# A decoder step on one core: six hidden groups of the third MLP block go from eight products of quarter matrices to seven, the cache stream's last steps move ahead of them, and its softmax is cut into portions

## The chip, the core and the metric

One Trainium2 chip, of which the program uses one core. The core has a matrix engine (TensorE, PE in the profile, with PEld for its weight loads), a vector engine (VectorE, DVE), an activation engine (ScalarE, ACT), a general engine (GpSimd, POOL) that also issues the gathers by index, and SyncE (SP), whose queue issues most plain DMAs. Each engine works through its own instructions in their order; semaphores tie the engines together. The metric is device time in microseconds for one execution. Three executions of the kernel before took 3270.63, 3259.38 and 3270.8 us, median 3270.63.

## The reference, cut to what matters

One inference step of a one-layer trunk. The new sequence (2048 tokens) and 64 sampled tokens (8 sequences of 8) go through one input projection, two kinds of attention, an output projection, a layer norm, an MLP and another layer norm:

```python
def _block_out(x, fox_h, m_h, og, mlstm_norm_w, w_o, ln1_g, ln1_b, w1, w2, ln2_g, ln2_b):
    ...
    x1 = _layer_norm(DN_ALPHA * x + mix, ln1_g, ln1_b)
    hid = jnp.square(jax.nn.relu(x1 @ w1))
    return _layer_norm(DN_ALPHA * x1 + hid @ w2, ln2_g, ln2_b)
```

`w1` is 1024 x 4096 and `w2` 4096 x 1024. The sampled tokens attend to a paged cache of 8192 keys and values for each of the 8 sequences:

```python
    s_past = jnp.einsum('bqhd,bkhd->bhqk', q, k_past).astype(jnp.float32) * scale
    s_past = s_past + Ln[..., :, None] + R[:, :, None, :]
    ...
    p = jax.nn.softmax(jnp.concatenate([s_past, s_new], axis=-1), axis=-1).astype(v_new.dtype)
    o = jnp.einsum('bhqk,bkhd->bqhd', p[..., :P], v_past) + jnp.einsum('bhqk,bkhd->bqhd', p[..., P:], v_new)
```

All is float32. The kernel splits each operand of a large product into a high and a low part and forms high x high, high x low and low x high: three matmuls for one product.

## The kernel before, in words

**Stages.** Phase A (to about 900 us) makes the input projection and the recurrent heads, phase B (to about 1320 us) the attention of the new sequence, phase O (to about 1560 us) the output projection and the first layer norm, phase C (to the end) the MLP. Phase C takes the tokens in four blocks: three of 512 tokens (tiles 0 to 3, 4 to 7, 8 to 11) in `phase_c`, and one of 512 tokens and the 64 sampled ones in `last_block`.

**A block of the MLP.** The 4096 hidden columns come in 16 groups `fc` of 256. `hidden(fc)` (L1560) loads and splits 256 columns of `w1`, forms 48 matmuls of 512 columns (2 halves of the group, 8 pieces of the inner dimension, 3 parts) and takes relu and square on ACT. `output([fc])` (L1578) forms the group's share of `hid @ w2`: 4 token tiles x 2 halves of the 1024 output columns x 2 halves of the group x 3 parts, again 48 matmuls of 512 columns, which DVE adds into the tiles' rows `y` (L1607). The two groups 14 and 15 are taken together, and the layer norm follows.

**Seven products.** `last_block` already uses another form for groups 0 to 13, the function `seven` (L1638), which stands unchanged in both kernels: the group's hidden values are seen as 2 x 2 quarters (two token halves, two hidden halves), the rows of `w2` as 2 x 2 quarters, and seven products of sums of quarters (Strassen's scheme in Winograd's form) replace eight. `sums(n)` forms the sums on POOL (four of 128x256, four of 128x512), `build(n)` splits them on ACT and DVE, `output(n)` forms the seven products, each 2 tiles x 3 parts = 6 matmuls of 512 columns, so 42 in place of 48, and `join()` adds the collected first product to the rows once at the end, in 12 DVE additions. `hidden(n)` there hands the low part of its second `w1` piece to POOL.

**The cache stream.** `sample_attention` is a generator: 295 steps `n` that gather a sequence's key pages (POOL), transpose them (DVE), form scores (`sQ` matmuls), take the softmax of a sequence once its scores are complete, transpose the weights into `PTs`, gather value pages, and form weights x values (`sO` matmuls, `pv_step`, L2120, 16 for each sequence, 8 matmuls each). For each `pv_step` two gathers of 512 KB fetch a pair of value pages (L2113). There are two places for such a pair: the tile `vt`, and `xr` (or `vx` in phase O); a place can be filled again when the `pv_step` that read it is done.

**What sets the order.** The stream is sewn into the other phases by `tick(us)` (L129): every unit of matrix work counts its nominal time, and for each `PACE_C` = 5 us of it in phases O and C one stream step is emitted, behind the work already emitted. In the third block, after `hidden(13)` and `output([12])`, a loop emits all steps that are left (L1627). `sampled()` (L1526) follows: it reads the stream's result back through HBM (`mixs` -> `dmix` -> `mxs`), splits it (`mhs`) and forms the output projection and first layer norm of the 64 sampled tokens, which the fourth block needs. A scheduler then arranges the emitted instructions on each engine; what it made is each engine's fixed order.

Of the kernel before, what the change touches and what calls it, by code (L numbers as in the profile page):

```python
# [10 lines left out]
F32 = mybir.dt.float32  # L11
F32R = mybir.dt.float32r
I32 = mybir.dt.int32
AF = mybir.ActivationFunctionType
# [7 lines left out]
PACE_B = float('inf')  # L22
PACE_C = 5
PACE_M = 2.3
D = 1024
# [27 lines left out]
def body(ctx, tc, I, O, stages):  # L53
# [111 lines left out]

    def layer_norm(x, np_, g, b, wk, tg, eng=None, by=None):
# [9 lines left out]
        (by or V).tensor_tensor(x, x, g[:np_], op=OP.mult)  # L176
        (eng or G).tensor_tensor(x, x, b[:np_], op=OP.add)
# [1333 lines left out]
    def phase_c():  # L1511
        es, es_h = ExitStack(), ExitStack()
        pc, ph = C["pc"], es_h.enter_context(tc.tile_pool(name="ph", bufs=1, side="right", reuse_waits="tile"))
# [33 lines left out]
        CB = [[0, 1, 2, 3], [4, 5, 6, 7], [8, 9, 10, 11], [12, 13, 14, 15, 16]]  # L1547
        def load(ci):
            for i, t in enumerate(CB[ci]):
                x1_turn(t, i, x1_row(t) if i == 3 else x1_load(t), lambda: ppc.tile([128, 4, 128], F32, name="px2", tag="ph", bufs=3))  # L1550
            vx["more"] = landing

        vx["more"] = landing
        for ci, blk in enumerate(CB[:3]):
# [4 lines left out]

            def hidden(fc):  # L1560
                w1p = C.pop("w1", None) or w1_pieces(fc)
                H[fc] = []
                for f in range(2):
                    h2 = ph.tile([128, 1024], F32R, name="h", bufs=4)
                    hh, hl = h2[:, 0:512], h2[:, 512:1024]
                    H[fc].append((hh, hl))
                    ps = ppc.tile([128, 512], F32, name="ph", tag="ph", bufs=3)
# [10 lines left out]
            def output(fcs):  # L1578
                w2p = [piece(w2[fc * 256 + k * 128:fc * 256 + k * 128 + 128].rearrange("(k p) c -> p k c", p=128)) for fc in fcs for k in range(2)]
                h = [x for fc in fcs for x in H.pop(fc)]  # L1580
                gb = gb2
                for t in blk:
# [8 lines left out]
                    both = 15 in fcs and t == blk[-1]  # L1591
                    pss = []
                    for hf, cs in enumerate(halves):
                        if not both or hf == 0:
                            todo = halves if both else [cs]
                            new = [ppc.tile([128, 512], F32, name="py", bufs=3) for _ in todo]
                            pss += new
# [14 lines left out]

            for fc in range(16):
                if fc == 14:
                    vx["more"] = None
                hidden(fc)
                if fc == 15:
                    take_back()
                    if ci == 2:
                        es_px.close()  # L1620
                        C["px"] = es_px.enter_context(tc.tile_pool(name="px", bufs=1, reuse_waits="tile"))
                        C["w"] = 576
                    load(ci + 1)
                if fc > 0:
                    output([14, 15] if fc == 15 else [fc - 1])
                if fc == 13 and ci == 2:
                    while acc[1] is not None:  # L1627
                        tick(100.0)
                    sampled()
                    gb2 = [ps_.tile([128, D], F32, name=f"{x}3", tag="vt", bufs=2) for x in "gb"]  # L1630
                    for v, x in zip(gb2, "gb"):
                        SY.dma_start(v, dap(I[f"ln2_{x}"], 0, [[0, 128], [1, D]]))
        es_h.close()
        es.close()
        last_block(w2, gb2)
        es_px.close()

# [119 lines left out]

    def last_block(w2, gb):
        es = ExitStack()
        ph = es.enter_context(tc.tile_pool(name="phs", bufs=1, side="right", reuse_waits="tile"))  # L1760
        ppl = es.enter_context(tc.tile_pool(name="ppl", bufs=1, space=PSUM, reuse_waits="tile"))
        T0, T1 = (12, 13), (14, 15)
# [93 lines left out]
def sample_attention(tc, I, O, ps_, pps, cst, ident, sqk, dnl, dR, dmix, dqb, vx, kx, pe, ring_a):  # L1856
# [180 lines left out]
    def softmax(b):  # L2037
# [20 lines left out]
        rp = z["rp"] = ps_.tile([128, 2, 5], F32, name="rp", bufs=2)  # L2058
        for u in range(4):
            for hg in range(2):  # L2060
                x = z["U"][u][:, hg].rearrange("p b k t -> p (b k t)")
                A.activation(x, x, AF.Exp, bias=m4[:, hg:hg + 1], accum_out=rp[:, hg, u:u + 1])
        for hg in range(2):
            A.activation(z["Sn"][:, hg], z["Sn"][:, hg], AF.Exp, bias=m4[:, hg:hg + 1], accum_out=rp[:, hg, 4:5])

    def softmax_new(b):

        z = state[b]
        rs = z["rs"] = ps_.tile([128, 2], F32, name="rs", bufs=2)
        V.tensor_reduce(rs, z["rp"], axis=AX.X, op=OP.add)  # L2070
        pn = z["pn"] = ps_.tile([8, 2, 32], F32, name="PTn", bufs=2)
# [14 lines left out]
    def weights(b, u, hg):  # L2086
# [6 lines left out]
        for f in range(4):  # L2093
            T.transpose(p[:, f], z["U"][u][:, hg, f].rearrange("p k t -> p (k t)"), ident)
        for f in range(4):
            (A.copy if f % 2 else V.tensor_copy)(PT[:, hg, f].rearrange("p g h q -> p h g q"),
                                                 p[:, f].rearrange("p (h g q) -> p h g q", g=4, q=8))

# [71 lines left out]
    def step(n):  # L2170
# [14 lines left out]
        if b is not None and b < 8:  # L2185
            softmax(b)
        due = (n - 38) // 2 if n > NA + 2 else (n - 39) // 2
        lead = 2
# [12 lines left out]
        if b is not None and b < 8:  # L2201
            softmax_sum(b)
        u = at(n, 37, 8)
        if u is not None and u < 32:
# [61 lines left out]
```

## Time and profile before

| | |
|---|---|
| median of three executions | 3270.63 us (3259.38 to 3270.8) |
| the profiled execution's own time | 3264.98 us |
| its span, first to last instruction | 3263.1 us |
| PE busy | 3174.9 us, 97% of the span, 20140 matmuls |
| DVE, ACT, POOL busy | 2230.5, 1393.6, 1049.9 us |
| mean granted TensorE clock | 0.990 |

The profile is one page and a trace behind it. A row on a group reads: line, engine, operation, output tile <- input tiles, shape, count | busy us, mean ns of one | idle time of the engine just before them, and what ended it. A row of a timeline reads: start us, duration us, engine, line, operation, and in brackets the idle time before it and its releaser. A row of a table of stages gives busy time and count of instructions for PE, PEld, DVE, ACT and POOL, then the granted clock, the DMA engines' busy share and GB/s. Matmul durations overlap (matmuls are pipelined), so the pace of PE is read from starts or from counts in a stretch. One execution's span and its own time differ by 1.9 us here.

### The profile page before, as it was taken

What the parts mean: (1) busy time and instruction counts of PE and PEld (TensorE: products, weight loads), DVE (VectorE), ACT (ScalarE), POOL (GpSimd) and SP (SyncE); (2) the same over time, 40 slices, a digit from 0 to 9 for tenths busy, and PEclk for the clock granted to TensorE, in tenths of its full rate; (3) what the DMA queues carried; (4) which work ended last, traced back from release to release, by engine and by line L of the source; (5) the groups of instructions that cost most, each with busy time, mean ns of one, the idle gap of its engine ahead of it and who ended that gap; (6) DMA issues with size and microseconds to landing.
All of it is one profiled execution on the core that took longest, in us unless ns stands there. A gap on an engine that the chain in (4) does not pass through costs nothing.

```text
span 3263.1 us, 54920 instructions
## 1 busy us (share of the span) xinstructions
PE 3174.9 (97%) x20140; PEld 2555.0 (78%) x20140; DVE 2230.5 (68%) x5239; ACT 1393.6 (43%) x2753; POOL 1049.9 (32%) x1171
## 2 busy tenths in 40 slices
PE   9999999999999999999999999999999999999998
PEld 8878787786777777777777777777777777799997
DVE  5857667666577777766566767666667545777777
ACT  4444244444377777412333333242423333454443
POOL 0011121432344444354333324323234210264441
PEclk9999999999999999999999999999999999999999
DMA  6565774977743224777686768776678645442221
GB/s 193 150 198 167 231 230 144 315 259 218 222 128 85 79 84 118 254 282 263 250 289 213 288 238 288 263 249 244 239 240 305 210 160 176 134 139 84 91 90 56
DMA packets 413845, 641.88 MB, mean 197 GB/s; under 512 B 83020, under 2 KB 295312, under 8 KB 412680
## 3 DMA queue, kind: packets, MB, share of 16 engines
q1 hardware_dynamic: 337320, 360.99, 36.4%
q0 software_dynamic: 74304, 270.57, 22.3%
q10 hardware_dynamic: 1952, 6.82, 0.6%
q8 instruction: 159, 2.61, 0.3%
q14 instruction: 110, 0.90, 0.1%
HBM read 585.43 MB, written 52.83 MB: 196 GB/s over the span
## 4 chain that ended last, share of the span: by engine, by line
PE 60%; DMA 5%; DVE 3%; issue 2%; POOL 1%; ACT 1%; SPq 0%; DVEq 0%; POOLq 0%; ACTq 0%
PE ph L157 7%; PE ph L158 7%; PE ph L159 7%; PE py L157 6%; PE py L159 6%; PE py L158 6%; PE po L1245 4%; PE pt L1228 4%; PE sO L2137 3%; PE pS L1187 2%; PE sQ L2025 2%; PE pS L1188 2%; DMA kT<-cache_k,idxK 2%; DMA xr<-cache_v,idxV 1%; PE pw L158 1%
## 5 line engine op out<-in xcount | busy, mean ns | idle before, releaser
L149 ACT ACTIVATE wh<-wr 128x1024 fp32r<-128x1024 f32 x268 | 277.6, 1056 | 538.2 <-PE py L159 299.8
L1996 POOL DMA_INDIRECT kT<-cache_k,idxK x256 | 262.3, 1025 | 741.1 <-PE sQ L2025 644.1
L2002 DVE STREAM_TRANSPOSE kT<-kT 128x512 f32<-128x512 f32 x512 | 330.2, 686 | 230.2 <-DMA kT<-cache_k,idxK 229.5
L157 PE MATMUL ph<-x1h,wh 128*128 128x512 f32 (+2 forms) x1280 | 453.5, 354 | 3.1 <-ACT xr L1664 2.1
L159 PE MATMUL ph<-x1h,wl 128*128 128x512 f32 (+2 forms) x1280 | 450.7, 354 | 6.0 <-DVE wl L152 6.0
L158 PE MATMUL ph<-x1l,wh 128*128 128x512 f32 (+2 forms) x1280 | 452.9, 354 | 0.0
L152 DVE TENSOR_TENSOR wl<-wr,wh 128x1024 fp32r<-128x1024 f32 x252 | 318.7, 1272 | 77.9 <-PE ph L159 45.8
L157 PE MATMUL py<-wh,h 128*128 128x512 f32 (+1 forms) x888 | 347.7, 395 | 0.8 <-DVE y L1807 0.3
L159 PE MATMUL py<-wh,h 128*128 128x512 f32 (+1 forms) x888 | 347.7, 392 | 0.0
L158 PE MATMUL py<-wl,h 128*128 128x512 f32 (+1 forms) x888 | 347.5, 392 | 0.0
L1607 DVE TENSOR_TENSOR y<-y,py 128x512 f32<-128x512 f32 x336 | 224.2, 677 | 142.6 <-PE py L159 140.6
L159 PEld LDWEIGHTS ph<-x1h,wl 128*128 128x128 f32 x1280 | 242.0, 189 | 38.9 <-DVE wl L152 7.1
L157 PEld LDWEIGHTS ph<-x1h,wh 128*128 128x128 f32 x1280 | 242.3, 189 | 38.1 <-ACT xr L1664 2.3
L158 PEld LDWEIGHTS ph<-x1l,wh 128*128 128x128 f32 x1280 | 242.1, 189 | 35.1 <-issue 2.5
L2113 POOL DMA_INDIRECT vt<-cache_v,idxV x156 | 160.6, 1030 | 291.0 <-PE sO L2137 252.1
L157 PE MATMUL pm<-whi,xhT 128*128 128x512 f32 (+2 forms) x648 | 235.7, 365 | 3.7 <-ACT acb L637 1.5
L158 PE MATMUL pm<-wlo,xhT 128*128 128x512 f32 (+2 forms) x648 | 230.7, 356 | 1.9 <-DVE wlo L152 1.9
L159 PE MATMUL pm<-whi,xlT 128*128 128x512 f32 (+2 forms) x648 | 230.6, 356 | 0.0
L157 PEld LDWEIGHTS py<-wh,h 128*128 128x128 f32 x888 | 167.1, 188 | 42.9 <-issue 7.8
L159 PEld LDWEIGHTS py<-wh,h 128*128 128x128 f32 x888 | 167.1, 188 | 36.2 <-issue 2.5
L158 PEld LDWEIGHTS py<-wl,h 128*128 128x128 f32 x888 | 167.1, 188 | 33.8 <-issue 2.9
L149 ACT ACTIVATE whi<-wra 128x1024 fp32r<-128x1024 f32 (+1 forms) x112 | 119.0, 1062 | 160.7 <-PE pm L159 105.6
(485 smaller groups left out, 7068.4 us busy)
## 6 DMA issues: line engine op xcount, KB each, us to landing
wr<-w SPq DMA_DIRECT2D x256, 512.0 KB
wra<-w_in SPq DMA_DIRECT2D x112, 512.0 KB
Rb<-dR SPq DMA_DIRECT2D x128, 128.0 KB
wr<-w_o SPq DMA_DIRECT2D x16, 512.0 KB
xr<-dmix SPq DMA_DIRECT2D x16, 512.0 KB
y<-x_prompt SPq DMA_DIRECT2D x16, 512.0 KB
dx<-y SPq DMA_DIRECT2D x16, 512.0 KB
qn<-dq SPq DMA_DIRECT2D x120, 64.0 KB
```

The lines of the kernel that those rows point to most:

```text
L149: last["ACT"] = A.activation(dst, src, AF.Copy, scale=scale)
L152: r = (eng or V).tensor_tensor(dst, src, hi.bitcast(F32), op=OP.subtract)
L157: T.matmul(ps, wh, xh, start=first, stop=False, skip_group_check=free)
L158: T.matmul(ps, wh, xl, start=False, stop=False, skip_group_check=free)
L159: last["PE"] = T.matmul(ps, wl, xh, start=False, stop=stop, skip_group_check=free)
L1228: T.transpose(pt[:, k], sc[i][0][k0 // 8][:, (k0 % 8 + k) * 128:(k0 % 8 + k + 1) * 128], ident)
L1245: last["PE"] = T.matmul(po[c:c + 64, q0:], z["vn"][:, k], PTs[k // 4][:, k % 4, q0:], start=k == same[0], stop=k == same[-1], skip_group_c ...
L1607: V.tensor_tensor(y, y, ps, op=OP.add)
L1996: G.indirect_dma_start(out=piece(n), out_offset=None, in_=ck, in_offset=IO(ap=idxK[:, b, j // 2, j % 2:j % 2 + 1], axis=0))
L2002: V.transpose(x, x)
L2113: vx["last"] = G.indirect_dma_start(out=vt.rearrange("p f c -> p (f c)"), out_offset=None, in_=cv, in_offset=IO(ap=idxV[:, b, (kt % 4) * 4 ...
L2137: after_ = T.matmul(po[r:r + 32], z["PT"][:, hg, 2 * f + g, pg].rearrange("p h q -> p (h q)"), vts[f][:, g, hg * 256:(hg + 1) * 256], star ...
```

## The change

Three things change.

1. **The third block.** A constant `SEVEN` = 8 is added. In the third block (`ci == 2`) the plain loop ends before group 8. The loop that emits what is left of the stream stands after `hidden(6)` and `output([5])` in place of `hidden(13)` and `output([12])`; `PACE_C` stays at 5. `sampled()` follows group 7's hidden part. Groups 8 to 13 ("nine to fourteen") go through `seven`; groups 14 and 15 are plain again, `join()` comes between. The fourth block's token transposes (`load(3, ...)`) use the PSUM pool `ppl`, which is opened here and handed to `last_block`.
2. **One-copy stream weights.** In `weights` four copies of 128x128 (two on DVE, two on ACT) from PSUM to `PTs` become one ACT copy of 128x512.
3. **Portioned exponentials.** `softmax(b)` took ten exponentials in one stream step; the new `exps(b, u)` takes two of 128x512 in each of four steps (and the two small ones with the first), and the sum over them (`rs`) moves to a later step.

`layer_norm` loses an unused parameter.

```diff
+SEVEN = 8
...
             for fc in range(16):
+                if ci == 2 and fc == SEVEN:
+                    break
...
-                if fc == 13 and ci == 2:
+                if ci == 2 and fc == SEVEN - 2:
                     while acc[1] is not None:
                         tick(100.0)
-                    sampled()
+            if ci < 2:
+                continue
+            run = seven(ph, blk, ys, C["x"], w2, lambda: es_l["ppl"])
+            sampled()
+            run["hidden"](SEVEN)
+            run["sums"](SEVEN)
+            output([SEVEN - 1])
+            es.close()
+            es_l["ppl"] = es_q.enter_context(tc.tile_pool(name="ppl", bufs=1, space=PSUM, reuse_waits="tile"))
+            for n in range(SEVEN + 1, 16):
+                if n < 15:
+                    h = run["build"](n - 1)
+                if n < 14:
+                    run["hidden"](n)
+                    run["sums"](n)
+                else:
+                    hidden(n, lambda f: pps.tile([128, 512], F32, name="ph", tag="sO" if f else "sX", bufs=1))
+                if n < 15:
+                    run["output"](n - 1, *h)
+                if n == 14:
+                    run["join"]()
...
+            load(3, lambda: es_l["ppl"].tile([128, 2, 512], F32, name="py", bufs=3)[:, 0].rearrange("p (k c) -> p k c", k=4))
+            output([14, 15], True)
...
+    def exps(b, u):
+        z = state[b]
+        for hg in range(2):
+            x = z["U"][u][:, hg].rearrange("p b k t -> p (b k t)")
+            A.activation(x, x, AF.Exp, bias=z["m4"][:, hg:hg + 1], accum_out=z["rp"][:, hg, u:u + 1])
...
-        for f in range(4):
-            (A.copy if f % 2 else V.tensor_copy)(PT[:, hg, f].rearrange("p g h q -> p h g q"),
-                                                 p[:, f].rearrange("p (h g q) -> p h g q", g=4, q=8))
+        A.copy(PT[:, hg].rearrange("p f g h q -> p f h g q"), p.rearrange("p f (h g q) -> p f h g q", g=4, q=8))
```

**Where instructions move.** On PE, the end of the stream before: the last four `pv_step`s of the last sequence, in two pairs. (`sO` are the stream's products, `vt` and `xr` the two halves of a value pair in each place, `ph` and `py` the MLP's products.)

```order
L2137 MATMUL sO_26424<-vt_27375,PTs_27502 32x256 x4
L2137 MATMUL sO_26424<-xr_27381,PTs_27502 32x256 x4
L2137 MATMUL sO_26424<-xr_27379,PTs_27502 32x256 x4
...
L2137 MATMUL sO_26424<-vt_27570,PTs_27502 32x256 x4
L2137 MATMUL sO_26424<-vt_27568,PTs_27502 32x256 x4
L2137 MATMUL sO_26424<-xr_27574,PTs_27502 32x256 x4
L2137 MATMUL sO_26424<-xr_27572,PTs_27502 32x256 x4
L2143 MATMUL sO_26424<-vns_26512,PTn_26506 32x256 x2
L157 MATMUL py_27758<-wh_27748,h_27471 128x512
```

The same place on PE in the changed kernel, from the seventh of the last sequence's sixteen `pv_step`s on:

```order
L2162 MATMUL sO_26248<-vt_26580,PTs_26551 32x256 x4
...
L160 MATMUL py_26884<-wh_26824,h_26420 128x512
L2162 MATMUL sO_26248<-xr_26586,PTs_26551 32x256 x4
L2162 MATMUL sO_26248<-xr_26584,PTs_26551 32x256 x4
L2121 MATMUL sT_26619<-ident_73,S_25390 128x128 x4
L2162 MATMUL sO_26248<-vt_26606,PTs_26612 32x256 x4
...
L2162 MATMUL sO_26248<-xr_26706,PTs_26673 32x256 x4
L2168 MATMUL sO_26248<-vns_26336,PTn_26330 32x256 x2
L2178 MATMUL sT_26730<-ident_73,os_26728 128x128 x2
L164 MATMUL py_26899<-wh_26902,mhs_26894 128x256
```

Before, 54 rows of `py` and `ph` stand between the two pairs (the first "..." above), and after the last one 145 more up to the first product that reads `mhs`. Now, behind the fifth and sixth `pv_step`, 24 rows of `py` stand ahead of the seventh and 6 ahead of the eighth; between the eighth and the sixteenth there are only transposes of weights (`sT`), and the sampled tokens' first product (`mhs`) follows the stream's last transpose at once.

On SP, around the round trip of the stream's result through HBM, before:

```order
L1368 DMA wr_28054<-w_o 128x4x256
L1368 DMA wr_28068<-w_o 128x4x256
L2243 DMA dmix_68<-mixs_2553 128x4x64
L1529 DMA mxs_27984<-dmix_68 128x8x64
L1368 DMA wr_28085<-w_o 128x4x256
L1368 DMA wr_28099<-w_o 128x4x256
L1368 DMA wr_28132<-w1 128x4x256
```

and in the changed kernel:

```order
L1369 DMA wr_26993<-w_o 128x4x256
L1369 DMA wr_27007<-w_o 128x4x256
L1652 DMA g3_28180<-ln2_g 128x1024
L1652 DMA b3_28181<-ln2_b 128x1024
L2276 DMA dmix_68<-mixs_2553 128x4x64
L1530 DMA mxs_26892<-dmix_68 128x8x64
L1369 DMA wr_27036<-w1 128x4x256
```

All eight pieces of `w_o` are now issued ahead of the round trip, and so are the vectors of the second layer norm, which are loaded into the place of `vt`; the next group's `w1` stays behind it.

More of the change, by code (lines that the diff above doesn't have):

```diff
@@ L1566, in hidden @@
                     H[fc].append((hh, hl))
[L1567 removed]
+                    ps = bank(f)
                     for k in range(8):
@@ L1592, in output @@
                     pss = []
+                    pair = es_l["ppl"].tile([128, 2, 512], F32, name="py", bufs=3) if wide else None
                     for hf, cs in enumerate(halves):
@@ L1595, in output @@
                             todo = halves if both else [cs]
-                            new = [ppc.tile([128, 512], F32, name="py", bufs=3) for _ in todo]
+                            new = [ppc.tile([128, 512], F32, name="py", bufs=3) for _ in todo] if pair is None else [pair[:, i] for i in range(2)][hf:hf + len(todo)]
                             pss += new
@@ L2202, in step @@
             softmax_sum(b)
+        b = at(n, 40, 32)
+        if b is not None and b < 8:
+            z = state[b]
+            z["rs"] = ps_.tile([128, 2], F32, name="rs", bufs=2)
+            V.tensor_reduce(z["rs"], z["rp"], axis=AX.X, op=OP.add)
         u = at(n, 37, 8)
```

43 lines of the change are left out of this document (20 added, 23 removed).

## The prediction

> **What bounds the kernel now.** I read the page first: what is busy, and the chain that ended last.
>
> ```profile
> PE 3174.9 (97%) x20140; PEld 2555.0 (78%) x20140; DVE 2230.5 (68%) x5239; ACT 1393.6 (43%) x2753; POOL 1049.9 (32%) x1171
> PE 60%; DMA 5%; DVE 3%; issue 2%; POOL 1%; ACT 1%; SPq 0%; DVEq 0%; POOLq 0%; ACTq 0%
> ```
>
> PE is busy for 97% of the span and no other engine comes near it. So time is won only by fewer matmuls or by removing some of PE's 88 us without work, and it is lost wherever PE's next instruction waits. Next the table of stages (PE, PEld, DVE, ACT, POOL busy; clock; DMA share; GB/s) over the part that the change rewrites: the third block's start, its middle, its end, and the fourth block.
>
> ```profile
> 2400.00:2500.00 100.00, 93.21 (x557) 72.35 (x556) 72.32 (x130) 34.23 (x50) 44.17 (x37) 0.97 0.81 285
> 2600.00:2700.00 100.00, 100.00 (x548) 77.58 (x545) 46.92 (x63) 32.76 (x48) 17.97 (x19) 1.00 0.52 172
> 2700.00:2800.00 100.00, 97.27 (x507) 78.75 (x506) 59.13 (x87) 35.92 (x46) 5.25 (x6) 1.00 0.56 180
> 2800.00:2900.00 100.00, 94.95 (x533) 83.70 (x533) 68.16 (x85) 45.88 (x77) 48.36 (x30) 0.98 0.39 130
> 2900.00:3200.00 300.00, 300.00 (x1802) 273.23 (x1801) 236.69 (x301) 144.57 (x261) 125.10 (x106) 1.00 0.28 88
> ```
>
> In 2600 to 2700 PE never stops although the stream still runs beside it. The chain of waits shows how the stream's last steps are spaced there (pairs of `pv_step`s; one pair holds PE 1.86 us, one step 0.93).
>
> ```profile
> 2695.28 1.86 PE sO L2137 x32
> 2730.32 1.86 PE sO L2137 x30
> 2744.64 1.86 PE sO L2137 x32
> ```
>
> 14 and 35 us of MLP work lie between pairs. That is the cover the value gathers have now.
>
> **Part 1a, the seven products: -8.** Each of six groups loses 48 - 42 = 6 matmuls of 512 columns, 36 in all. Their price is the pace of PE, not the 392 ns of a row. First and last of 18 matmuls in a stretch without waits:
>
> ```profile
> 2590.13 0.39 PE L159 MATMUL ph<-x1h,wl 128*128 128x512 f32 x1
> 2593.98 0.39 PE L158 MATMUL ph<-x1l,wh 128*128 128x512 f32 x1
> ```
>
> 3.85 / 17 = 0.2265 us, so 36 are worth 8.2 us. The additions this costs elsewhere are covered if the other engines keep up. The fourth block already runs this way with more columns; its collecting addition shows the period of a group.
>
> ```profile
> 3152.38 1.22 DVE L1740 TENSOR_TENSOR kT<-kT,py 128x1024 f32<-128x1024 f32 x1 [1.00 <-PE py L159]
> 3176.73 1.22 DVE L1740 TENSOR_TENSOR kT<-kT,py 128x1024 f32<-128x1024 f32 x1 [1.00 <-PE py L159]
> ```
>
> The period is 24.35 us with PE always busy. From the last table row, DVE works 236.7 / 300 x 24.35 = 19.2 us of it, ACT 11.7, POOL 10.2. A third-block group now has 90 matmuls, 20.4 us, and none of the sampled tokens' additions. So DVE stays under 19.2 of 20.4 us and covers itself. Without that cover the group would take 24.35 us, 6 x 3.95 = 24 us more.
>
> **Part 1b, the end of the stream: +29.** The stream's pace is unchanged, but the loop that empties it now stands seven groups earlier. PE's order says what that means. After the fifth and sixth `pv_step` of the last sequence come 24 `py` rows, the seventh, 6 `py` rows, the eighth, and then eight more with nothing but transposes between. PE works in order and has nothing else to do there. Each `pv_step` waits for two gathers that may start only when the step two places earlier has freed its place. The price of that loop comes from POOL's timeline and the value cache's landings in 2590 to 2745 us:
>
> ```profile
> 2598.44 0.64 PE L2137 MATMUL sO<-vt,PTs 128*32 128x256 f32 x8
> 2590.69 0.94 POOL L2113 DMA_INDIRECT xr<-cache_v,idxV  x1 [0.30 <-issue]
> 2591.93 0.94 POOL L2113 DMA_INDIRECT xr<-cache_v,idxV  x1 [0.30 <-issue]
> 2599.38 1.04 POOL L2113 DMA_INDIRECT vt<-cache_v,idxV  x1 [6.51 <-PE sO L2137]
> DMA to landing us min/median/max: 3.9/6.5/8.7
> ```
>
> PE's products end at 2599.08 and POOL starts at 2599.38: 0.30. The second gather follows 1.24 later, lands 6.5 after its start, and the step takes 0.93: 8.97 us a loop. The two places run side by side, the second 2 x 1.24 = 2.5 us behind. From the end of the fifth step to the end of the sixteenth that is 5 loops + 2.5 = 47.4 us. PE has work for 30 x 0.2265 + 11 x 0.93 + 3 transposes of some 0.6 = 18.8 of it. The wait is 28.6 us. With the fastest landing, 3.9, it is 15.6; with the slowest, 8.7, it is 39.6. I take the median: four gathers at a time were in flight in those rows too.
>
> On the landing there is a rule in the Trainium skill, "DMA: Bandwidth & Descriptors", section "Anatomy of one DMA — SWDGE (gpsimd) path": about 2.0 us fixed plus bytes at 436 GB/s. For 512 KB that gives an estimate of 3.2 us, below the fastest row here; the median row, 6.5, disagrees.
>
> **Part 1c, the round trip through HBM: +6.** After the last step the result goes DVE, PE, DVE, HBM, back, ACT, DVE, and PE's next instruction is the first product on `mhs`. Before, 145 rows of other matmuls stood between. Rows before:
>
> ```profile
> 2747.96 0.48 DVE L2146 TENSOR_SCALAR os<-sO,rl 128x256 f32<-128x256 f32 x1
> 2768.88 0.38 PE L2153 MATMUL sT<-ident,os 128*128 128x128 f32 x2
> 2772.37 0.87 DVE L2158 TENSOR_REDUCE mixs<-sT 64x8 f32<-64x16 f32 x8
> 2773.26 0.37 SPq L2243 DMA_DIRECT2D dmix<-mixs  x1
> 2775.29 0.37 SPq L1529 DMA_DIRECT2D mxs<-dmix  x1
> L149 ACT ACTIVATE mhs<-mxs x1: 633/633/633, 2779.5 to 2779.5; 128x512 fp32r<-128x512 f32 x1
> 2781.20 0.68 DVE L152 TENSOR_TENSOR mhs<-mxs,mhs 128x512 fp32r<-128x512 f32 x1
> 2781.94 0.39 PE L163 MATMUL py<-wh,mhs 128*128 128x256 f32 x1 [1.76 <-DVE mhs L152]
> ```
>
> The write takes 2.03 us (SP's second issue waited for it). The read lies between the same 2.03 and the 4.2 us to ACT's start; I take 2.5, nearer the write. 0.48 + 0.38 + 0.87 + 2.03 + 2.5 + 0.63 + 0.68 = 7.6, with hand-overs 8. Before, 1.8 of it were open: +6 (5 to 9; the two 512 KB vector loads ahead of it on SP could add). ACT and SP stand still with it: `w1` of the next group is issued only behind the read, hidden by 64 products on `mhs`. I add 1 (0 to 3).
>
> **Part 1d, the granted clock: +6.** The row 2400 to 2500 above holds two waits, in the list of PE's waits:
>
> ```profile
> PE px L1403 <- DMA xr<-dx: 6.4, 2, 5.6
> PE sO L2137 <- DMA vt<-cache_v,idxV: 5.8, 3, 4.2
> ```
>
> One wait of 5.6 us there goes with a clock of 0.97, so 3 us of pace lost beside the wait. The new place has five waits of 4 to 6 us and one of 8 in a row. The little work between them (12 us) can lose at most its own length, and the first products after it 3: I take 6 (3 to 12). The Trainium skill, "TensorE: Matmul & The Clock Gate", section "HAM oscillation — how this bites in real kernels", says that DMA waits beyond some 3.4 us throttle PE each time; by it the upper half of that range would hold and the sum would be some 4 us more. The row with 0.97 agrees that a wait of 5.6 us throttles.
>
> **Part 1e, the border to the fourth block: +3.** The ten token transposes now use three double banks of one pool and stand together ahead of the last output products, and DVE has 12 more additions of 0.68 us just ahead. Before, other matmuls stood between them. Bounds: 0 (all within slack) to 8 (all 12 in the way); the row of a late token load above, 5.6, is between. I take 3.
>
> **Parts 2 and 3, copies and exponentials: -2.**
>
> ```profile
> L2096 DVE COPY PTs<-sT 128x128 f32<-128x128 f32 x128 | 35.6, 278 | 37.2 <-PE sT L2094 26.8 <-ACT PTs L2096 10.2
> L2096 ACT COPY PTs<-sT 128x128 f32<-128x128 f32 x128 | 33.6, 263 | 215.4 <-DVE PTs L2096 215.3
> L1231 ACT COPY wr<-pt 128x512 f32<-128x512 f32 (+1 forms) x102 | 52.3, 552 | 12.6 <-PE pt L1228 11.8
> PE sO L2137 <- DVE PTs L2096: 2.8, 1, 2.8
> PE sT L2094 <- ACT PTs L2096: 2.0, 1, 2.0
> PE sQ L2025 <- ACT PTs L2096: 1.7, 1, 1.7
> ```
>
> DVE loses 35.6 us; ACT trades 33.6 for 64 x 0.55 = 35. Both have slack (68% and 43% busy), so only PE's waits count: 2.8 + 2.0 + 1.7 = 6.5 us hang on these copies. The gain lies between 6.5 and a loss of 3, since one ACT copy now stands between two transposes; I take 2. The exponentials are the same in number; dividing them shortens ACT's longest block, which no PE wait above names.
>
> **Sum**, on the profiled execution's own 3265.0 us: -8.2 + 28.6 + 6 + 1 + 6 + 3 - 2 = +34.4, so 3299.4; I say 3300. The median of the runs shown lies 5.6 above that execution, within their scatter, so I leave the number as it is.
>
> **Rivals.** (A) The gathers land at their quickest because fewer transfers compete: loop 6.4 us, wait 15.6, clock loss 4, total 3285. For it: the DMA share of 0.52 in 2600 to 2700 and the 3.9 us row; against it: four gathers crowd each other. By the Trainium skill's rule named above ("DMA: Bandwidth & Descriptors") a loop would be 3.3 us shorter than with the median row, an estimate of 3284 for the whole, near this case. (B) The third block's seven-product groups are held by DVE or POOL and take the fourth block's 24.35 us: +24, total 3324. Against it: the fourth block shows PE busy 300 of 300. (C) Not slower: the stall finds cover, since the scheduler's rows around the emptied stream suffice. One mechanism: 47.4 us of gather loops need some 126 more matmuls (28.6 / 0.2265) between the steps; then 3265.0 - 8.2 + 3 - 2 = 3258. It decides once that many stand there, and PE's order shows 30. (D) The stream is further along than I count, with no loop left: same 3258; the order excludes most of it.
>
> **Chances.** The forecast's own case (3291 to 3311) 0.60, A 0.18, B 0.09, C and D 0.08, something in the earlier stream 0.05. About 0.5%, some 16 us, is what a measurement of this kernel can tell from no change. Slower by more than that takes the forecast, A and B, 0.88; within it C and D and a strong A, 0.09; faster 0.03, since even every gain at its bound (8.2 + 6.5) stays at 14.7. The range: 3281 (below A) to 3320 (slow landings, clock at its bound), leaving out B's upper half.
>
> **What would show it.** In the changed profile: PE waits on `sO` <- DMA of `cache_v` of some 25 to 35 us in one stretch of the third block, in steps near 9 us per pair; one wait of 7 to 9 us at `mhs`; clock well under 1.00 there; then group periods of 20.4 us. Wrong if PE is busy through that stretch, if the loops take 6 us, or if the groups take over 21.8 us.

## The result, and the profile after

The changed kernel takes 3299.76 us (median of six, 3290.71 to 3306.31); the kernel before takes 3267.73 us beside it (3259.38 to 3270.8). The ratio is 1.010, with a 95% interval of 1.0086 to 1.0114: slower by 32 us, where 3300 was forecast. The profiled execution took 3300.83 us, its span is 3299.1.

The page's first lines and its chain, as they stand after the change:

```profile
PE 3179.0 (96%) x20104; PEld 2553.8 (77%) x20104; DVE 2244.0 (68%) x5158; ACT 1411.5 (43%) x2708; POOL 1121.7 (34%) x1225
PE 71%; DMA 10%; issue 9%; DVE 6%; POOL 2%; ACT 1%; SPq 0%; DVEq 0%; POOLq 0%; ACTq 0%
```

36 matmuls are gone, and yet PE is busy 4 us longer, in a span that is 36 us longer. DMA's share of the chain of waits that ended last has doubled (5% before). The four largest of PE's waits from 2600 to 2720 us (line and releaser: us in total, times, longest) name the place:

```profile
PE sO L2162 <- DMA vt<-cache_v,idxV: 9.1, 4, 3.9
PE py L164 <- DVE mhs L153: 7.2, 1, 7.2
PE sO L2162 <- DMA xr<-cache_v,idxV: 7.0, 5, 2.1
PE ph L160 <- DVE wl L153: 5.6, 1, 5.6
```

Three of the four rows were forecast: the stream's products wait for their gathers (`vt` and `xr`), and the sampled tokens' first product (`mhs`) waits for the round trip. The fourth was not in this form. The timeline of PE shows the steps, here the seventh, ninth and sixteenth `pv_step` of the last sequence, the last transpose of the result and the first product on it:

```profile
2629.35 1.07 PE L2162 MATMUL sO<-vt,PTs 128*32 128x256 f32 x16
2638.83 1.94 PE L2162 MATMUL sO<-vt,PTs 128*32 128x256 f32 x16 [3.94 <-DMA vt<-cache_v,idxV]
2667.07 1.93 PE L2162 MATMUL sO<-xr,PTs 128*32 128x256 f32 x16 [1.17 <-DMA xr<-cache_v,idxV]
2670.59 0.69 PE L2178 MATMUL sT<-ident,os 128*128 128x128 f32 x2 [0.59 <-DVE os L2171]
2678.47 0.58 PE L164 MATMUL py<-wh,mhs 128*128 128x256 f32 x1 [7.19 <-DVE mhs L153]
```

From the fifth step's end (2622.4) to the sixteenth's (2669.0) pass 46.6 us; 47.4 were forecast. The same `pv_step` (16 rows in the trace) takes 1.07 us as the seventh, and 1.94 as the ninth and 1.93 as the last, where the granted clock is 0.50. The table of stages (columns as in the prediction) gives it for the stretch, for what follows, and for the clean middle of the seven-product groups:

```profile
2622.00:2671.00 49.00, 30.89 (x234) 14.74 (x226) 6.33 (x9) 4.35 (x6) 19.91 (x20) 0.65 0.79 257
2671.00:2703.00 32.00, 24.58 (x133) 21.33 (x131) 20.79 (x33) 12.58 (x14) 10.04 (x7) 0.84 0.47 144
2713.00:2830.00 117.00, 117.00 (x514) 96.17 (x513) 90.00 (x108) 53.23 (x71) 59.41 (x46) 1.00 0.35 113
2850.00:2870.00 20.00, 16.04 (x72) 12.54 (x71) 14.64 (x22) 12.77 (x22) 6.43 (x4) 0.83 0.28 91
```

The clock can be placed more closely. These are the four stretches from 2570 to 2946 us in which it is 0.50:

```profile
2637.00:2681.40 44.40, 22.39 (x155) 10.04 (x156) 2.85 (x11) 2.83 (x4) 11.23 (x12) 0.50 0.66 212
2705.30:2712.10 6.80, 2.82 (x7) 2.24 (x8) 6.75 (x6) 1.54 (x4) 4.51 (x3) 0.50 0.27 72
2858.90:2862.30 3.40, 3.37 (x16) 2.52 (x14) 2.61 (x5) 2.43 (x5) 2.19 (x2) 0.50 0.44 137
2865.70:2869.10 3.40, 3.40 (x9) 2.66 (x8) 1.56 (x2) 0.91 (x2) 0.00 (x0) 0.50 0.00 0
```

The kernel before has one over the same part of the program:

```profile
2863.00:2866.40 3.40, 3.40 (x18) 3.40 (x17) 3.06 (x2) 1.83 (x7) 3.40 (x2) 0.50 0.50 147
```

The first stretch is unbroken, although after its first wait (3.94 us) none is longer than 2.81 until the one of 7.19 at `mhs`, and 1.1 to 3.0 us of work stand between two of them.

In the groups of seven products PE never stops (117.00 of 117.00): no other engine holds them. At the border to the fourth block it does, and the clock falls again, to 0.83.

The fourth wait, 5.6 us, is on the split of the next `w1`. The timeline of DVE has it, with the operation ahead:

```profile
2701.73 1.21 DVE L153 TENSOR_TENSOR tl<-kT,th 128x1024 fp32r<-128x1024 f32 x1
2702.96 6.27 DVE L153 TENSOR_TENSOR wl<-wr,wh 128x1024 fp32r<-128x1024 f32 x1
```

And the timeline of POOL over the same stretch:

```profile
2701.88 3.28 POOL L178 TENSOR_TENSOR y<-y,kT 64x1024 f32<-64x1024 f32 x1 [3.82 <-DVE y L177]
2705.12 2.34 POOL L153 TENSOR_TENSOR wl<-wr,wh 128x1024 fp32r<-128x1024 f32 x1
2707.42 0.72 POOL L1710 TENSOR_TENSOR sr<-xr 128x256 f32<-128x256 f32 x1
2708.10 1.71 POOL L1708 TENSOR_TENSOR sr<-xr 128x256 f32<-128x256 f32 x1
```

A subtraction of two inputs that took 1.21 us just before takes 6.27, while POOL runs operations of two inputs without a break. It ends at 2709.23, 1.1 us after the end of POOL's third, and POOL's fourth takes 1.71 where the median of its kind is 0.75.

### The profile page after: what moved, and what is told of

It is laid out like the page before. It is cut to its first block, busy times and chain, and to the rows that moved or that the text cites. A ratio compares the mean times of both kernels' runs of the same rounds, so it can differ in the third digit from the quotient of the medians.

```text
span 3299.1 us, 54665 instructions
## 1 busy us (share of the span) xinstructions
PE 3179.0 (96%) x20104; PEld 2553.8 (77%) x20104; DVE 2244.0 (68%) x5158; ACT 1411.5 (43%) x2708; POOL 1121.7 (34%) x1225
## 4 chain that ended last, share of the span: by engine, by line
PE 71%; DMA 10%; issue 9%; DVE 6%; POOL 2%; ACT 1%; SPq 0%; DVEq 0%; POOLq 0%; ACTq 0%
PE ph L160 5%; PE ph L158 5%; PE ph L159 5%; PE pm L158 5%; PE py L158 5%; DMA kT<-cache_k,idxK 5%; PE pm L159 5%; PE pm L160 5%; PE py L160 5%; PE py L159 5%; PE po L1246 4%; PE pt L1229 3%; PE sQ L2049 3%; PE sO L2162 2%; PE pS L1188 2%
## 5 line engine op out<-in xcount | busy, mean ns | idle before, releaser
L150 ACT ACTIVATE wh<-wr 128x1024 fp32r<-128x1024 f32 (+1 forms) x268 | 275.2, 1046 | 429.0 <-PE py L160 155.2
L153 DVE TENSOR_TENSOR wl<-wr,wh 128x1024 fp32r<-128x1024 f32 (+1 forms) x246 | 316.0, 1294 | 78.9 <-PE ph L160 43.1
L158 PE MATMUL py<-wh,h 128*128 128x512 f32 x828 | 324.2, 398 | 3.3 <-DVE y L1607 1.7
L160 PE MATMUL py<-wh,h 128*128 128x512 f32 x828 | 324.1, 392 | 0.1
L159 PE MATMUL py<-wl,h 128*128 128x512 f32 x828 | 324.1, 392 | 0.0
L1609 DVE TENSOR_TENSOR y<-y,py 128x512 f32<-128x512 f32 x288 | 190.2, 676 | 146.3 <-PE py L160 145.5
L158 PEld LDWEIGHTS py<-wh,h 128*128 128x128 f32 x828 | 155.8, 188 | 45.9 <-issue 7.8
L153 DVE TENSOR_TENSOR wlo<-wra,whi 128x1024 fp32r<-128x1024 f32 (+1 forms) x112 | 136.6, 1221 | 79.0 <-ACT whi L150 78.4
L1772 DVE TENSOR_TENSOR y<-y,py 128x512 f32<-128x512 f32 (+1 forms) x245 | 163.9, 711 | 35.0 <-PE py L160 34.9
```

The costliest lines, as they stand in the source:

```text
L150: last["ACT"] = A.activation(dst, src, AF.Copy, scale=scale)
L153: r = (eng or V).tensor_tensor(dst, src, hi.bitcast(F32), op=OP.subtract)
L158: T.matmul(ps, wh, xh, start=first, stop=False, skip_group_check=free)
L159: T.matmul(ps, wh, xl, start=False, stop=False, skip_group_check=free)
L160: last["PE"] = T.matmul(ps, wl, xh, start=False, stop=stop, skip_group_check=free)
L1609: V.tensor_tensor(y, y, ps, op=OP.add)
```

## The experiments

My theory, in four parts: the stream's end, emitted seven groups early, leaves PE with gather loops, in which a place is freed, filled by two gathers and used again (the main loss); the round trip behind it is a bare wait; the split is held up by POOL; and the border takes back what the seven products win. The rivals were that the seven-product groups lose the time, that the softmax's portions do, and that all these are one chain in which a mended stretch only makes the next one wait. The runs were made on several chips, and on two of them the kernel before itself takes 3349 and 3326 us, so each total is read by its ratio to the kernel before on its own chip.

**1. The stream's end alone.** The kernel before, with the emptying loop and the sampled tokens moved as in the change, all groups plain, the softmax as before.

```diff
-                if fc == 13 and ci == 2:
+                if fc == 6 and ci == 2:
                     while acc[1] is not None:
                         tick(100.0)
+                if fc == 7 and ci == 2:
                     sampled()
+                if fc == 13 and ci == 2:
                     gb2 = ...
```

> The kernel before with the stream emptied behind hidden(6) and the sampled tokens' layer behind hidden(7), as in the change, but all sixteen groups plain and the old softmax. Theory (the loss is the end of the stream without cover, the round trip through HBM behind it and the half clock with both; the seven products win 8): before + 29 + 6 + 6 + 1, about 3310 us (3302 to 3318), slower than the change itself by some 8. Rival 1 (the seven-product groups cost time themselves, through DVE and POOL, and the end of the stream costs little): 3290 or less, at least 10 under the change.

Measured: 3299.71 us against 3264.73, ratio 1.0108 (1.0082 to 1.0134). PE's three largest waits from 2600 to 2700 us:

```profile
PE sO L2139 <- DMA vt<-cache_v,idxV: 17.7, 4, 6.3
PE py L163 <- DVE mhs L152: 8.0, 1, 8.0
PE sO L2139 <- DMA xr<-cache_v,idxV: 2.9, 3, 1.3
```

Moving the end of the stream costs as much by itself (35 us) as the whole change (32). That is less than the 42 of the expectation, whose lower bound of 3302 was missed. So the seven products, which were to win 8 us, and the softmax's parts together win nothing measurable beside it.

**2. The softmax alone.** The kernel before with parts 2 and 3 of the change: the one ACT copy, `exps(b, u)`, and the later sum.

> The kernel before with the one-copy weights and the portioned exponentials alone. Theory: PE's waits on these copies were 6.5 us in all, so 3266 us (3259 to 3271), no difference that can be measured. Rival 2 (the profile of the change reaches the end of phase A 9.3 us later than before, and this comes from the one ACT copy that now stands between two transposes): 3275 us or more.

> The kernel before with the one-copy weights and the portioned exponentials alone, once more, beside the other two: 0.9975 as measured first, 0.996 to 0.999. Here it tells whether anything of the third block's rewriting is worth keeping.

Measured: 0.9975 (0.9962 to 0.9988) on one chip, 1.0023 (1.0004 to 1.0041) on another. The two intervals lie on both sides of 1. The first is a little below the range expected, the second outside it. What these parts do is smaller than the difference between chips, and its sign stays open.

**3. A denser stream.** The changed kernel with `PACE_C = 4.2`.

> The change with PACE_C 4.2 in place of 5, so that the stream's steps are all emitted by hidden(6) and nothing is left for the emptying loop; on PE some 290 rows then stand between the stream's last transpose and the sampled tokens' first product. Theory: all of the wait, the round trip and the half clock go, 3260 us (3254 to 3270), 7 under the kernel before. Rival 3 (a denser stream waits for its gathers elsewhere in phases O and C): 3280 or more. Rival 1: 3280 or more as well, since the seven-product groups are as they are.

Measured: 3276.12 us, ratio 1.0034 (1.002 to 1.0049). PE's waits from 2560 to 2690 us are only these:

```profile
PE py L164 <- DVE mhs L153: 1.8, 1, 1.8
PE ph L158 <- ACT wh L150: 1.4, 1, 1.4
```

The gather loops are gone, and so is 0.7% of the time. But 3260 was expected, and 3280 by the rivals; the time lies between. The constant also sets the pace in phase O. The first product of the MLP phase starts at 1582.4 us there and at 1558.2 after the change. 80 more rows of the stream stand on PE in that phase, which only moves them; but PE's waits in it rise from 5.4 to 16.6 us, and the two longest are none that the changed kernel has:

```profile
PE sT L2121 <- ACT S L2090: 6.7, 1, 6.7
PE sQ L2049 <- DVE kT L2026: 3.3, 1, 3.3
```

So this mend paid at another place, and run 7 takes the denser pace for the MLP phase alone.

**4. More places.** The changed kernel, with three more pairs of tiles for value pages (in the ring of key tiles, free by then) in the stream's last part.

```diff
-        place = 0 if 0 not in vx["live"] else 1
+        place = next(i for i in range(5) if i not in vx["live"] and (i != 1 or vx["more"]))
...
+        if vx.get("tail"):
+            return vx["next"] < 128 and len(vx["live"]) < (5 if vx["more"] else 4)
...
+        if n >= 259:
+            vx["tail"] = True
```

> The change with three more places for value pairs in the last steps of the stream (in the key ring, which is free by then); the same instructions otherwise, and the same end without cover. Theory (the wait is the loop of a place: freed, gathered, landed, used): five places in flight, the last six pairs come 2.5 to 3.3 us apart, the wait falls from 29 to some 7 us and the half clock with it, 3274 us (3266 to 3284). Rival 4 (the gathers are bound by what the DMA engines move, not by a place's loop): above 3290, since the same 10 MB must land in the same stretch.

Measured: 3279.72 us, ratio 1.0052 (1.0036 to 1.0068). PE's two largest waits from 2590 to 2690 us:

```profile
PE py L164 <- DVE mhs L153: 7.6, 1, 7.6
PE sO L2165 <- DMA vt<-cache_v,idxV: 5.8, 1, 5.8
```

Nine waits on gathers have become one, with the steps at the same place in the program and the same bytes moved. What bound them was the return of a place, as the prediction's loop has it. The round trip's wait is untouched.

**5. Free banks at the border.** The fourth block's transposes take the stream's two PSUM banks, which are free by then.

```diff
-            load(3, lambda: es_l["ppl"].tile([128, 2, 512], F32, name="py", bufs=3)[:, 0].rearrange("p (k c) -> p k c", k=4))
+            load(3, lambda banks=iter("XO" * 5): pps.tile([128, 512], F32, name="px2", tag="s" + next(banks), bufs=1).rearrange("p (k c) -> p k c", k=4))
```

> The changed kernel with one difference: the fourth block's ten token transposes take the stream's two free PSUM banks in turn instead of the double banks that the output products also use. Theory (the border costs some 8 to 10 us there, not 3, because five transposes and their splits stand together with no products between them): with its own banks other products stand between the transposes again, the border waits of 7.9 us fall to about 2 to 4, and the time is 5 to 8 us under the changed kernel's 3299.8, 3292 to 3295. Rival (the border costs what the prediction said, 3 us, and the missing gain is lost inside the seven-product groups): no more than 2 us under it, 3298 to 3300.

Measured: ratio 1.0072 (1.0048 to 1.0096), on a chip where the kernel before takes 3348.92. The absolute times of the expectation can't be compared there, and the interval overlaps that of the change (1.0086 to 1.0114), so the total alone does not show a gain. Run 6, on the same chip, has the border as the change left it. From the last `ph` of the third block to the first of the fourth block's group 3 it takes 93.8 us, and this kernel 87.6: 6.2 less, within the 5 to 8 expected. But 2.3 of it is 10 products that stand ahead of this stretch here and in it there, and the waits did not fall to 2 or 4 us. The largest from 2915 to 3005 us are these:

```profile
PE px L1404 <- DVE x1l L153: 5.2, 3, 2.7
PE ph L158 <- DVE x1l L153: 2.0, 1, 2.0
PE py L158 <- DVE y L1772: 0.8, 1, 0.8
```

Over the stretch the waits are 7.2 us where run 6 has 8.0. What fell is the time at half clock: run 6 has 17.0 us of it in the stretch, in three pieces, this kernel 10.2 in one. So the shared banks were part of the border's cost, though not by the length of the waits. The waits that are left all name DVE. The same place in run 7's kernel (20 us there) shows how full it is:

```profile
2890.00:2910.00 20.00, 15.86 (x82) 12.61 (x80) 19.27 (x32) 7.53 (x12) 9.70 (x6) 1.00 0.29 90
```

DVE works 19.27 of 20.00 us: the layer norm, the additions of the last two groups, the splits of the new tokens and of the fourth block's first weights meet there. That its load is the cause is not shown: in run 8's kernel, with plain groups, DVE works 18.19 of the 20 us from 2900 on, and PE never stops.

**6. POOL out of the way.** The changed kernel, with the norm's last addition and the low part of one piece of `w1` on DVE instead of POOL.

```diff
-            layer_norm(y[:64], 64, *vecs(1), pc, "1")
+            layer_norm(y[:64], 64, *vecs(1), pc, "1", V)
...
-            w1p = w1_pieces(n, G)
+            w1p = w1_pieces(n, *(() if n == SEVEN and not more else (G,)))
```

> The changed kernel with two POOL operations moved to DVE: the last addition of the sampled tokens' layer norm, and the low part of the second w1 piece of the first seven-product group. Theory (DVE's split of w1 took 6.27 us in place of 1.22 because POOL ran additions over the same memory without a break): the split takes 1.2 to 2.5 us, the wait of 5.57 us before the first product on it falls below 2, total 3 to 5 us under 3299.8, about 3295. Rival (the split was slow for a reason that has nothing to do with POOL, such as the transfers in flight): it still takes over 4 us, and the total is 3299 or, with DVE's two more operations, 3301.

Measured: ratio 1.0075 (1.0047 to 1.0103), an interval that holds the change's 1.010; the total shows nothing by itself. The timeline of DVE at the split:

```profile
2785.86 1.21 DVE L153 TENSOR_TENSOR wl<-wr,wh 128x1024 fp32r<-128x1024 f32 x1
2787.00 0.41 DVE L153 TENSOR_TENSOR h<-xr,h 128x256 fp32r<-128x256 f32 x1
```

POOL's over the same stretch:

```profile
2783.15 0.73 POOL L1710 TENSOR_TENSOR sr<-xr 128x256 f32<-128x256 f32 x1
2787.45 3.37 POOL L153 TENSOR_TENSOR wl<-wr,wh 128x1024 fp32r<-128x1024 f32 x1 [3.57 <-ACT wh L150]
```

With POOL idle from 2783.9 to 2787.5 the split takes 1.21 us. PE's wait on it is gone (run 5, on the same chip and with POOL as before, has it: 4.9 us). DVE does two operations more and is still done sooner: from the first `ph` of group 9 to the last `ph` of the block pass 146.8 us, and 152.5 in run 5. And now POOL's split overlaps DVE's work, and takes 3.37 us in place of 2.34. In the Trainium skill, "SBUF — State Buffer", section "Who interferes with whom", a DVE operation with two inputs in SBUF and a POOL operation that reads SBUF exclude each other: whichever comes second stands still until the first is done. The runs agree in kind, both ways round. In size the changed kernel goes beyond one operation: DVE got no turn through three of POOL's, as the end of its split shows (above).

**7 and 8. The stream denser in the MLP phase only; the same with plain groups.** Run 5's kernel with the pace 4.4 from the MLP phase on (`acc[2] = 4.4` before `phase_c()`); and the same stream with all groups of the third block plain.

> The changed kernel with the free banks at the border, and the stream's pace of 5 us per step made 4.4 from the start of the MLP phase on (not in the phase before). The stream then ends 80 rows of PE ahead of the first product on its result. Theory (the stream's uncovered end and the border are all that the change lost, and the seven products do win their 8 us): 3258.4 of the portioned softmax alone, less 8.2, plus 2 to 3 at the border, plus 0 to 4 for the denser stream: 3253 to 3258. Rival (the seven-product groups win nothing, or the denser stream costs what it wins): 3263 or more.

> The stream exactly as in the 4.4 us pace (its end again 81 rows of PE ahead of the first product on its result, portioned softmax), but all sixteen groups of the third block as eight products, with the border to the fourth block as in the kernel before. It differs from the 4.4 us kernel in the seven products and their border alone. Theory (the six groups win about 8 us, and their border gives back 3 to 8 of them): the 4.4 us kernel is 0 to 5 us faster than this one, which comes to a ratio of 0.996 to 0.998 to the kernel before. First rival (the whole 8 us arrive): the 4.4 us kernel is 7 us or more faster. Second rival (the groups win nothing at all): it is over 2 us slower than this one.

> The 4.4 us pace with seven products and free banks at the border, once more, beside the kernel before, the same with plain groups, and the softmax alone on one chip. It came to a ratio of 0.9957. Theory: 0.994 to 0.997, faster than the softmax alone by 2 to 6 us. Rival (the softmax alone holds the whole gain): within 2 us of it or slower.

Measured: the first 0.9957 (0.9936 to 0.9979) on one chip and 0.9985 (0.9968 to 1.0001) on another; the plain one, on this other chip, 0.9978 (0.996 to 0.9996); the softmax alone there 1.0023. So a stream whose end is covered gives back all that the change lost. But the two kernels that differ in nothing but the seven products and their border are equal within their scatter: 3320.2 (3314.19 to 3325.55) and 3319.92 us (3308.22 to 3329.32). The theory's 0 to 5 us ends at its lower bound. The first rival, all 8 us arriving, is out; the second, a loss of over 2 us, is not excluded by ten executions each. PE's waits of the plain one, from its first `ph` of group 9 through the border, are one row:

```profile
PE ph L157 <- ACT rs L1668: 2.0, 2, 1.1
```

The three largest of the seven-product one over the same part of the program:

```profile
PE px L1404 <- DVE x1l L153: 5.1, 3, 2.7
PE ph L158 <- DVE x1l L153: 2.2, 1, 2.2
PE py L158 <- DVE y L1772: 0.8, 1, 0.8
```

From the first `ph` of group 9 to the border's end the plain kernel takes 148.3 + 81.6 = 229.9 us, the seven-product one 145.7 + 86.8 = 232.5. The stretch has 40 rows fewer (4 stand ahead of it), which at 0.2265 us should have taken 9.1 away. The waits give back 7 of them, the clock behind them (0.83 granted from 2910 to 2930 us there) some 2 more, an estimate, and the slower rows of products of sums 0.8 (below); the last 2 us I can't assign.

**9. The sampled tokens later.** In the changed kernel `sampled()` is emitted after group 8's hidden products, its sums and `output([7])` in place of before them.

> The changed kernel with the sampled tokens' projection emitted after the hidden products of group 8 and the output of group 7 in place of before them: 48 rows of PE, some 11 us, stand between the stream's last step and the first product on its result. Theory (the 8 us round trip through HBM is a wait because nothing stands in front of it): the wait of 7.2 us at that product goes to under 1, and with it the time falls 5 to 8 us, a ratio of 1.0075 to 1.0085 where the change had 1.010. Rival (the stretch is bound by something else, and the wait comes back elsewhere, at the split of the next w1 or at the end of the block): the wait goes, the ratio stays at 1.0095 or more.

Measured: ratio 1.0109 (1.0072 to 1.0146), on the chip that takes 3326 before. The wait at the first product on `mhs` is gone; its timeline has

```profile
2751.99 0.69 PE L2178 MATMUL sT<-ident,os 128*128 128x128 f32 x2 [0.59 <-DVE os L2171]
2764.78 0.28 PE L164 MATMUL py<-wh,mhs 128*128 128x256 f32 x1
```

with other products in the 12 us between. In its place PE waits 2.9 + 2.2 us for the splits of `w_o`, in five pieces. The ratio lies in the rival's range, and its interval is too wide to exclude the theory's. By the waits, 7.2 us became 5.1: most of the wait came back at another place, as the rival has it.

**10. All mends together.** Places, POOL's operations, banks and the later `sampled()`, with the stream at its pace of 5.

> The changed kernel, its stream at the same 5 us pace, with four mends together: three more places for value pairs in the stream's last part, the two POOL operations moved to DVE, free banks for the fourth block's token transposes, and the sampled tokens' projection behind the hidden products of group 8. Theory (the change's loss of 32 us is made of four separate stretches: the gather loops, the split held up by POOL, the border, the round trip): the gains add up, 20 + 5 + 6 + 6 = 37 us, and the ratio to the kernel before is 0.997 to 1.001. Rival (they are one chain, and a stretch that is mended lets the next one wait as long): 1.003 or more.

Measured: 3271.49 us against 3266.43, ratio 1.0019 (1.0007 to 1.0031). PE's waits from 2570 to 2700 us:

```profile
PE py L165 <- DVE wl L153: 4.1, 4, 1.7
PE ph L160 <- DVE wl L153: 1.1, 1, 1.1
PE py L164 <- ACT wh L150: 0.7, 1, 0.7
```

The ratio lies 0.1% above the range expected, and its interval just reaches the rival's bound: of 0.0100 lost, 0.0081 is back. The stretches add up, nearly. What stays is the waits above, 5.9 us, most of them for the splits of `w_o`, and 8.2 us at the border, all of which name DVE: 14.1 us together.

## Why the prediction was right, and where it was not

The total was right, 3300 for 3299.76, and the main term carries it. Some of the others had wrong sizes that cancelled. Point by point:

- **1b, the end of the stream, +28.6: right in the loop and its number, and lucky in its parts.** 46.6 us for 47.4, less 18.8 of own work, is 27.8. Its make-up was different. The gathers landed in 4.3, 5.6 and 7.9 us (fastest, median, slowest; 6.5 was taken), 0.9 quicker than I had it; a step took 1.94 us, 1.0 slower than the 0.93 taken. That the two cancel is luck. From one step's end to the next in the same place passed 7.8 to 8.6 us in the last six loops and 10.4 and 11.6 in the two before, for 8.97. Of the 27.8 some 17.6 are waits and 10 are slow work; so the sign of 25 to 35 us of waits for gathers did not come, they are 16.1. Rival A, quick landings, did not come; nor did the estimate of 3.2 us by the Trainium skill ("DMA: Bandwidth & Descriptors", section "Anatomy of one DMA — SWDGE (gpsimd) path"), which lies below the fastest landing here.
- **1d, the clock, +6: mis-sized, and the reasoning failed.** I added the slow work inside the stretch on top of the loop. But the loop is set by the gathers, and slow work is part of it. An estimate from the rows at 0.50 above: half of PE's busy time in them was lost, 16.0 us, and 1.7 in the kernel before. Of the 16.0, 8.9 lie inside the loops (up to 2669.0), 3.7 behind them (to 2681.4, and from 2705.3), and 3.4 at the border. So the term is 3.7, where 6 was forecast.
- **1c, the round trip, +6: right.** 8.5 us from the end of the stream's last product (2670.0) over the transpose to the first product on `mhs`, 7.19 of them an open wait where 1.76 stood before: +5.4.
- **1c's rest, `w1` behind it, +1 (0 to 3): failed.** I looked for a late load on SP. The load of the piece in question was in time: ACT started on its high part at 2701.88 without a wait. The split was held up by POOL, and cost 5.6. Run 6 shows it.
- **1a, the seven products, -8.2: right in the groups, and not kept.** PE is busy 117 of 117 us in them, so rival B is out. A row of products of sums starts a little slower (0.232 us for 0.2265; the first and last of six are below, from the timeline of PE in run 4's kernel), which for the 144 of them leaves 7.4 us of the 8.2.

```profile
2734.62 0.40 PE L158 MATMUL py<-th,h 128*128 128x512 f32 x1
2735.78 0.39 PE L160 MATMUL py<-th,h 128*128 128x512 f32 x1
```

  The collecting additions follow one another in 21.1 us on average, not 20.4 (first and last of five below, from the timeline of DVE in the changed kernel: 84.39 / 4), though PE has no wait in the stretch; they do not stand at the same place of every group.

```profile
2752.76 1.21 DVE L1765 TENSOR_TENSOR kT<-kT,py 128x1024 f32<-128x1024 f32 x1
2837.15 1.22 DVE L1765 TENSOR_TENSOR kT<-kT,py 128x1024 f32<-128x1024 f32 x1
```

- **1e, the border, +3 (0 to 8): mis-sized.** From the third block's last `ph` to the fourth block's group 3 the kernel before takes 85.3 us, the changed one 90.7: +5.4. The kernel before has 5.1 us of waits and 3.4 us at half clock there; against run 1, which takes 81.9, it is +8.8. That DVE's 12 additions make it is not shown: of the changed kernel's waits from 2830 to 2920 us, 10.2 in all, ACT is named for 6.7 and DVE for 3.5. In runs 7 and 8 the border and the slower rows cancel the seven products' whole gain; the prediction's -8.2 + 3 left 5.2 of it.
- **Parts 2 and 3, -2: within what was measured,** between -0.25% and +0.23%, and no better than that.
- **C and D, cover found:** out; PE had the 30 products between the steps that its order showed.

By stretches: up to the third block's group 6 the changed kernel is 4.3 us ahead, behind the fourth block's group 3 it gains 0.9. Between, 41.2 are lost, of which the terms above explain 27.8 + 5.4 + 5.6 + 5.4 - 7.4 = 36.8. The clock behind the loops (3.7) and the wait of 0.6 ahead of the last transposes of the result bring it to 41.1. The same stretch can be added up another way. PE's waits are 41.4 us there and 7.9 before, half clock takes 16.0 and 1.7 (the estimate above), 31 rows fewer are worth 7.0, and the slower rows 0.8: 33.5 + 14.3 - 7.0 + 0.8 = 41.6.

That the total fell on the forecast is partly luck: `w1` and the border came out 7 us dearer than I had them, the clock 2.3 cheaper, and the changed kernel reached the third block's group 6 4.3 us early.

No version here beats the kernel before clearly. The best, with the denser stream in the MLP phase, is 0.1 to 0.4% faster, with either kind of groups, and one of the three intervals reaches 1.

## What to carry to other kernels

A background stream has a drain time of its own: steps left, divided by places, times gather loop. Emit its end only where that many matmuls still stand between the steps; more places or an earlier start are worth more than a saving of products behind it. Products that are saved on the full engine can be paid where the scheme ends: look at which engines' work meets there, and for half clock behind the waits. And look at which engine runs beside a split that PE needs next: giving POOL a share of DVE's operations can make DVE slower than doing them itself, as run 6 shows here.

## What was not expected of the hardware

A DVE subtraction of 128x1024 with both inputs in SBUF, 1.21 us when alone, took 6.27 us beside POOL's operations that followed each other without a gap, and 1.21 again when POOL stood still. On the two slower chips DVE stood idle in the MLP's first two blocks without any work that the trace names as the cause. The group of additions into the rows, from 1600 to 2400 us, for the kernel with the softmax's parts alone on the faster chip (the last column is the idle time before them):

```profile
L1607 DVE TENSOR_TENSOR y<-y,py 128x512 f32<-128x512 f32 x217 | 142.7, 675 | 91.7 <-PE py L159 91.3
```

The same kernel and view on a slower chip:

```profile
L1607 DVE TENSOR_TENSOR y<-y,py 128x512 f32<-128x512 f32 x200 | 131.0, 676 | 160.1 <-PE py L159 86.2 <-remote 41.6 <-PE ph L159 24.1
```

The operation takes 0.675 us on both, but 41.6 us of idle time have a releaser outside this core's known queues, and PE's waits in these two blocks rise from 10.5 to 50.6 us. What it is stays open.
